# Four gates of the third branch computed among the mixer's last products, and a scan paced by 15, 13 and 9 dense products

## The chip, the core and the metric

The kernel runs on one core of a Trainium2 chip. The metric is the device time of one execution in microseconds. Every duration below comes from one execution taken by the hardware profiler, in which each engine's instructions have a start and a length. TensorE is PE in the profile, VectorE DVE, ScalarE ACT, GpSimd POOL, and SyncE, which only issues transfers here, SP.

## The reference, cut to what matters

The program is a trunk of two layers over 512 positions of width 1024. Each layer is a half-step feed-forward block, a mixer, and a second half-step feed-forward block. The change lies in the mixer:

```python
h = _rmsnorm(x, mix_norm[l])
proj = h @ w_in[l]
y_a = _deltanet_branch(...) @ w_proj_a[l]
y_b = _pooling_branch(...) @ w_proj_b[l]
y_c = _dilated_branch(...) @ w_proj_c[l]
gates = jax.nn.sigmoid(h @ w_gate[l] + b_gate[l]).reshape(B_, S, N_BRANCHES, D)
merged = gates[:, :, 0] * y_a + gates[:, :, 1] * y_b + gates[:, :, 2] * y_c
x = x + merged @ w_out[l]
```

The three gates depend on h alone, so they can be computed at any time of the mixer. Branch A is a gated delta rule in 8 chunks of 64 positions, in both directions: a scan, in which each chunk reads a state, solves a small triangular system, and writes the state.

## The kernel before, in words

Activations are kept transposed: 8 blocks of 128 features by 512 positions. Every large product is done in three passes, since each operand is split into a high part (fp32r) and the remainder: `gemm` (L222 to L239) issues for each inner block of 128 a product of high by high, high by low and low by high, L232, L234 and L236, and so an output block with 8 inner blocks takes 24 products of 128x128 by 512 columns. These are the dense products. The weights come by DMA from SP's queue (L199) and are split by `split` (L182 on ACT, L183 on DVE). The results land in three accumulators in turn, each free again when DVE has read it.

In the mixer the order of work is that of the code, as a scheduler places it on each engine:

- first the projections and preparations of the deltanet, then the 8 gates of branch A, which stay in the tiles `mg`, then 16 gates of branches B and C, each written to the DRAM tensor `gd` (L1053), then four products for z;
- then, by the string `ORDER`, the attention's projections `p0`, `p1`, `p2` with rotary additions on POOL (`rope`, L794 to L803), the attention groups `a0` to `a2`, the pooling `P`, the product `y` of branch A, and the attention's merge `m`;
- then the blocks: 8 for branch B (weights wpb, 12 products each) and 8 for branch C (wpc, 6 products each). Each reads its gate back from `gd` (L1086), multiplies on DVE (L1088) and adds to `mg` on POOL (L1089);
- then `mg` is split into the tiles MR (L182, L183), and the 8 wo products of 24 products follow (L1100), which need all eight MR.

The scan's small products don't stand by themselves. They are a list of steps, X.steps, and `step`, called after every dense product, takes the next one from the list when enough dense products have gone by: `DPACE`, 14, for each. The steps start in the middle of the gates (`MG`): five of preparation, then for each of the 8 chunks read (products L672, results used by L679 on DVE and L688 on ACT), solve (L699; L706 on ACT, L708 on DVE) and write (L716; L726 on DVE). Behind them come `out_block` (L735, L737, L740), `out_norm` (L747 to L753, with a square root and so a load of ACT's function table, L261) and `out_head` (transposes L759, then L762 and a split). In `a0` the scores (L869) go through L881, L884, L886 and the exponentials L889 before they are transposed (L899).

## Time and profile before

| what | value |
|---|---|
| median of 3 runs | 2594.52 us (2593.94 to 2596.76) |
| the profiled execution | 2593.36 us |
| its span, first to last instruction | 2591.6 us |
| granted TensorE clock, mean | 0.998 |
| PE busy | 2565.7 us, 99% |
| DVE busy | 1469.1 us, 57% |
| ACT busy | 1008.9 us, 39% |
| POOL busy | 162.3 us, 6% |

Busy time of PE is the union of durations that overlap: a dense product lasts 0.39 us, and the next may start before it ends. So the starts of the products tell more than their lengths. In a row of the timeline the bracket tells how long the engine sat idle before the instruction, and what ended that.

### The profile page before, as it was taken

To read this page: it belongs to the slowest core of one execution; us is meant where nothing else is said; L and a number is where in the kernel's file an instruction comes from. 1 tells how busy PE (TensorE), PEld (TensorE's weight loads), DVE (VectorE), ACT (ScalarE), POOL (GpSimd) and SP (SyncE) were. 2 spreads that over 40 slices of the span, in tenths; PEclk is the share of its full clock that TensorE was granted. 3 is DMA by queue.
4 is the path that set the end of the run, shared out by engine and by line. 5 is a ranking of instruction groups with operands and counts; after the bars stand their busy time and mean duration, and the time that the engine had idled before them with its cause. 6 is when DMAs were issued, how large, how long until landed. Compare 5 with 4: busy or idle time off the path is not lost.

```text
span 2591.6 us, 34050 instructions
## 1 busy us (share of the span) xinstructions
PE 2565.7 (99%) x13064; PEld 2102.1 (81%) x13064; DVE 1469.1 (57%) x2698; ACT 1008.9 (39%) x1948; POOL 162.3 (6%) x117
## 2 busy tenths in 40 slices
PE   9999999999999999999999999999999999999998
PEld 7888887888887788888888888878888877888887
DVE  6444349956757754444444443599466487544433
ACT  5333234564434333333233332355644343333322
POOL 1000000000230300000000000000012203000010
PEclk9999999999999999999999999999999999999999
DMA  4223333332432522233322333323334325322232
GB/s 154 97 98 96 112 111 98 99 118 87 122 103 74 171 91 96 97 98 96 100 96 94 97 101 114 112 89 106 107 98 121 92 74 175 98 96 94 94 98 82
DMA packets 96979, 269.36 MB, mean 104 GB/s; under 512 B 15664, under 2 KB 20144, under 8 KB 96816
## 3 DMA queue, kind: packets, MB, share of 16 engines
q1 hardware_dynamic: 75280, 229.39, 28.2%
q10 hardware_dynamic: 21536, 37.80, 4.5%
q8 instruction: 102, 1.67, 0.3%
q14 instruction: 61, 0.50, 0.1%
HBM read 243.99 MB, written 16.86 MB: 101 GB/s over the span
## 4 chain that ended last, share of the span: by engine, by line
PE 95%; DVE 2%; ACT 1%; issue 1%; DMA 1%; POOL 0%; SPq 0%; DVEq 0%; ACTq 0%
PE acc L236 29%; PE acc L232 29%; PE acc L234 29%; PE m L914 1%; PE m L672 1%; PE m L699 1%; PE m L716 1%; PE m L735 1%; PE m L899 1%; PE m L869 0%; DMA raw<-in_wo_dram 0%; DVE wl L183 0%; PE m L647 0%; PE m L1023 0%; PE m L608 0%
## 5 line engine op out<-in xcount | busy, mean ns | idle before, releaser
L182 ACT ACTIVATE wh<-raw 128x512 fp32r<-128x512 f32 (+1 forms) x870 | 539.1, 620 | 1193.0 <-PE acc L234 1068.7
L234 PE MATMUL acc<-xl,wh 128*128 128x512 f32 x2400 | 941.9, 393 | 1.4 <-DVE xl L1126 1.2
L236 PE MATMUL acc<-xh,wl 128*128 128x512 f32 x2400 | 941.7, 392 | 1.4 <-DVE wl L183 1.4
L232 PE MATMUL acc<-xh,wh 128*128 128x512 f32 x2400 | 941.1, 392 | 1.3 <-ACT wh L182 1.1
L183 DVE TENSOR_TENSOR wl<-raw,wh 128x512 fp32r<-128x512 f32 (+1 forms) x870 | 606.0, 697 | 578.1 <-ACT wh L182 572.1
L232 PEld LDWEIGHTS acc<-xh,wh 128*128 128x128 f32 x2400 | 450.9, 188 | 99.1 <-issue 3.0
L234 PEld LDWEIGHTS acc<-xl,wh 128*128 128x128 f32 x2400 | 450.9, 188 | 96.9 <-DVE xl L1126 3.9
L236 PEld LDWEIGHTS acc<-xh,wl 128*128 128x128 f32 x2400 | 451.0, 188 | 96.7 <-DVE wl L183 2.3
L232 PE MATMUL acc<-r,wh 128*128 128x512 f32 x970 | 379.8, 392 | 5.8 <-DVE f L1088 4.5
L234 PE MATMUL acc<-r,wh 128*128 128x512 f32 x970 | 378.5, 391 | 3.5 <-DVE r L183 3.5
L236 PE MATMUL acc<-r,wl 128*128 128x512 f32 x970 | 377.7, 390 | 0.0
L232 PEld LDWEIGHTS acc<-r,wh 128*128 128x128 f32 x970 | 182.1, 188 | 46.5 <-ACT r L182 4.4
L234 PEld LDWEIGHTS acc<-r,wh 128*128 128x128 f32 x970 | 182.2, 188 | 42.5 <-DVE r L183 5.8
L236 PEld LDWEIGHTS acc<-r,wl 128*128 128x128 f32 x970 | 182.1, 188 | 37.5
L298 DVE TENSOR_TENSOR t<-acc,R 128x512 f32<-128x512 f32 x88 | 60.9, 692 | 132.2 <-PE acc L236 132.2
L294 DVE TENSOR_TENSOR f<-acc,R 128x512 f32<-128x512 f32 x88 | 60.9, 692 | 128.1 <-PE acc L236 128.0
L182 ACT ACTIVATE r<-t 128x512 fp32r<-128x512 f32 x96 | 60.6, 632 | 132.6 <-DVE t L299 127.4
L183 DVE TENSOR_TENSOR r<-t,r 128x512 fp32r<-128x512 f32 x96 | 66.2, 692 | 60.8 <-ACT r L182 60.8
L579 POOL MEMSET r<- 128x1024 f32 x2 | 1.9, 953 | 1107.7 <-PE acc L236 1107.7
L365 DVE SCALAR_TENSOR_TENSOR f<-t,cw,f 128x512 f32<-128x512 f32 x96 | 69.2, 741 | 0.0
L295 ACT ACTIVATE f<-f 128x512 f32<-128x512 f32 x88 | 55.6, 632 | 23.0 <-DVE f L294 22.9
L299 DVE TENSOR_TENSOR t<-t,f 128x512 f32<-128x512 f32 x88 | 60.4, 686 | 1.3 <-ACT f L295 1.3
(282 smaller groups left out, 1744.6 us busy)
## 6 DMA issues: line engine op xcount, KB each, us to landing
raw<-in_win_dram SPq DMA_DIRECT2D x76, 512.0 KB, 3.7
raw<-in_wgt_dram SPq DMA_DIRECT2D x48, 512.0 KB, 3.3
raw<-in_f2g_dram SPq DMA_DIRECT2D x44, 512.0 KB, 3.2
raw<-in_f2u_dram SPq DMA_DIRECT2D x44, 512.0 KB, 3.3
raw<-in_f1g_dram SPq DMA_DIRECT2D x43, 512.0 KB, 3.3
raw<-in_f1u_dram SPq DMA_DIRECT2D x43, 512.0 KB, 3.3
raw<-in_f1d_dram SPq DMA_DIRECT2D x32, 512.0 KB, 3.5
raw<-in_f2d_dram SPq DMA_DIRECT2D x32, 512.0 KB, 3.4
```

The costliest lines, as they stand in the source:

```text
L182: S.activation(h, raw, AF.Copy)
L183: V.tensor_tensor(out=l, in0=raw, in1=f32(h), op=ALU.subtract)
L232: PE.matmul(acc, a, h, start=(k == 0), stop=False)
L234: PE.matmul(acc, a, l, start=False, stop=False)
L236: last = PE.matmul(acc, b, h, start=False, stop=(k == nk - 1))
L294: V.tensor_tensor(out=g1, in0=g, in1=R, op=ALU.mult)
L295: S.activation(g1, g1, AF.Silu)
L298: V.tensor_tensor(out=u1, in0=u, in1=R, op=ALU.mult)
L299: V.tensor_tensor(out=u1, in0=u1, in1=g1, op=ALU.mult)
L365: V.scalar_tensor_tensor(out=a, in0=cp[:, j:j + T], scalar=w[:, j:j + 1], in1=a, op0=ALU.mult, op1=ALU.add)
L672: PE.matmul(p1[:, h * P:(h + 1) * P], KQ[h][:, c * P:(c + 1) * P], X.ST[:, di * T + h * P:di * T + (h + 1) * P], start=True, stop=True)
L699: PE.matmul(P3[di][r0:r0 + 64, h * P:(h + 1) * P], M[di][r0:r0 + 64, o:o + 64], U[b][r0:r0 + 64, di * T + h * P:di * T + (h + 1) * P], sta ...
```

## The change

Of the 16 gates of branches B and C the first 12 are computed and written to `gd` as before. The last four, of branch C, blocks 4 to 7, are computed in the last loop, each just in front of the wpc block that uses it, and stay in the tile `t`. The two loops over the blocks become one loop over the string `YORD`, in the same sequence. The pace of the scan is given with each step: 15 dense products ahead of a read, 13 ahead of a solve, 9 ahead of a write, and 14 for all others.

```diff
-DPACE = 14
+NG = 4
+YORD = "10 11 12 13 14 15 16 17 20 21 22 23 24 25 26 27"
+DPACE = {"read": 15, "solve": 13, "write": 9}
...
-    gd = pd.tile([2 * NB, P, T], F32, name="gd")
+    gd = pd.tile([NB + NG, P, T], F32, name="gd")
...
-                if ln[1] >= ln[2]:
+                if ln[1] >= (ln[0][0][0] or ln[2]):
                     ln[1] = 0
-                    ln[0].pop(0)()
+                    ln[0].pop(0)[1]()
...
-        def add(*fs):
-            X.steps.append(lambda: [f() for f in fs])
+        def add(*fs, n=14):
+            X.steps.append((n, lambda: [f() for f in fs]))
...
-                add(lambda s=s: read(s))
-            add(lambda s=s: solve(s))
+                add(lambda s=s: read(s), n=DPACE["read"])
+            add(lambda s=s: solve(s), n=DPACE["solve"])
...
-        for d in range(2 * NB):
+        for d in range(NB + NG):
...
-        for br, yy, wp in ((0, YB, "wpb"), (1, YC, "wpc")):
-            for d in range(NB):
-                t = tf()
-                nc.scalar.dma_start(t, gd[br * NB + d])
-                y = gemm(A[wp][l][d], yy)
-                V.scalar_tensor_tensor(out=t, in0=t, scalar=1.0, in1=y, op0=ALU.add, op1=ALU.mult)
-                G.tensor_tensor(out=mg[d], in0=mg[d], in1=t, op=ALU.add)
+        for br, d in [(int(c[0]), int(c[1])) for c in YORD.split()]:
+            yy, wp = ((YB, "wpb"), (YC, "wpc"))[br - 1]
+            t = tf()
+            if br == 2 and d >= NG:
+                gate(2, d, t)
+            else:
+                nc.scalar.dma_start(t, gd[(br - 1) * NB + d])
+            y = gemm(A[wp][l][d], yy)
+            V.scalar_tensor_tensor(out=t, in0=t, scalar=1.0, in1=y, op0=ALU.add, op1=ALU.mult)
+            G.tensor_tensor(out=mg[d], in0=mg[d], in1=t, op=ALU.add)
```

How instructions move is shown at three places of the first layer. In the new file lines up to the pace's are 2 higher and those of the last loop 5 (L183 is L185, L1088 is L1093).

The first place is DVE at the last wpc blocks. `f` is a gate's tile, `wl` a low part of weights, `r<-mg` the split of the merged tiles. Before, from the fourth block on:

```order
L1088 SCALAR_TENSOR_TENSOR f_7536<-f_7536,acc_7538 128x512
L183 TENSOR_TENSOR wl_7608<-raw_7609,wh_7607 128x256
L183 TENSOR_TENSOR r_7638<-mg_3771,r_7638 128x512
L183 TENSOR_TENSOR wl_7625<-raw_7626,wh_7624 128x256
L1088 SCALAR_TENSOR_TENSOR f_7553<-f_7553,acc_7555 128x512
L1088 SCALAR_TENSOR_TENSOR f_7570<-f_7570,acc_7572 128x512
L183 TENSOR_TENSOR r_7641<-mg_3809,r_7641 128x512
L183 TENSOR_TENSOR wl_7666<-raw_7667,wh_7665 128x512
L1088 SCALAR_TENSOR_TENSOR f_7587<-f_7587,acc_7589 128x512
L183 TENSOR_TENSOR r_7644<-mg_3847,r_7644 128x512
```

And after, where L1042 takes a gate from its accumulator:

```order
L1042 TENSOR_TENSOR f_7414<-acc_7415,R 128x512
L185 TENSOR_TENSOR wl_7507<-raw_7508,wh_7506 128x256
L1093 SCALAR_TENSOR_TENSOR f_7414<-f_7414,acc_7452 128x512
L185 TENSOR_TENSOR wl_7523<-raw_7524,wh_7522 128x512
L185 TENSOR_TENSOR r_7638<-mg_3923,r_7638 128x512
L185 TENSOR_TENSOR wl_7541<-raw_7524,wh_7540 128x512
L1042 TENSOR_TENSOR f_7467<-acc_7468,R 128x512
L185 TENSOR_TENSOR wl_7560<-raw_7561,wh_7559 128x256
L1093 SCALAR_TENSOR_TENSOR f_7467<-f_7467,acc_7505 128x512
L185 TENSOR_TENSOR wl_7576<-raw_7577,wh_7575 128x512
L185 TENSOR_TENSOR r_7641<-mg_3961,r_7641 128x512
```

Between two multiplies stand now a gate's accumulator and its two weight splits of 512 columns, and one split of mg.

The second place is ACT behind the scan, where the sums of squares of the last blocks (`ocol`) are followed by the load of the function table for the square root. Before:

```order
L740 ACTIVATE t_5681,ocol_3770<-r_4651 128x128 x4
L182 ACTIVATE wh_5826<-raw_5828 128x512
L740 ACTIVATE t_5704,ocol_3770<-r_4652 128x128 x4
L761 DMA t_5780<-zd 128x512
L261 ACT_TABLE_LOAD
L261 ACTIVATE rs_994_5731<-ov_5727 128x16
L794 ACTIVATE f_5746<-acc_5648 128x512
```

And after:

```order
L742 ACTIVATE t_5633,ocol_3770<-r_4651 128x128 x4
L184 ACTIVATE wh_5785<-raw_5769 128x512
L742 ACTIVATE t_5656,ocol_3770<-r_4652 128x128 x4
L837 ACTIVATE r_5570<-m_5667 64x128
L836 ACTIVATE t_5571<-m_5668 64x128
L839 ACTIVATE r_5570<-m_5667 128x3x128
L263 ACT_TABLE_LOAD
L263 ACTIVATE rs_991_5698<-ov_5694 128x16
L184 ACTIVATE wh_5854<-raw_5856 128x512
```

The square root stood beside the rotary step of the keys; now it stands behind the copies of the first half of the values V.

The third place is PE at the transposes of the deltanet's output (L759, after the change L761), of which the two heads' banks `m` are filled in turn. Before:

```order
L236 MATMUL acc_5756<-xh_95,wl_5798 128x512
L759 MATMUL m_5775<-ident,r_4651 128x128
L759 MATMUL m_5786<-ident,r_4651 128x128
L232 MATMUL acc_5756<-xh_96,wh_5797 128x512
L234 MATMUL acc_5756<-xl_104,wh_5797 128x512
L236 MATMUL acc_5756<-xh_96,wl_5798 128x512
L232 MATMUL acc_5756<-xh_97,wh_5797 128x512
L759 MATMUL m_5775<-ident,r_4651 128x128
```

And after:

```order
L761 MATMUL m_5729<-ident,r_4651 128x128
L761 MATMUL m_5740<-ident,r_4651 128x128
L234 MATMUL acc_5766<-xh_90,wh_5767 128x512
L761 MATMUL m_5729<-ident,r_4651 128x128
L761 MATMUL m_5740<-ident,r_4651 128x128
L236 MATMUL acc_5766<-xl_98,wh_5767 128x512
L238 MATMUL acc_5766<-xh_90,wl_5768 128x512
L832 MATMUL m_5753<-ident,f_5751 64x128
```

They now come where `p0` ends and `p1` begins, among the transposes of V (L830 to L833, now L832 to L835).

## Rows read from the trace of the kernel before

**Rows 1.** The page: the busy time of each engine, and the engines' shares of the chain that ended last.

```profile
PE 2565.7 (99%) x13064; PEld 2102.1 (81%) x13064; DVE 1469.1 (57%) x2698; ACT 1008.9 (39%) x1948; POOL 162.3 (6%) x117
...
PE 95%; DVE 2%; ACT 1%; issue 1%; DMA 1%; POOL 0%; SPq 0%; DVEq 0%; ACTq 0%
```

**Rows 2.** The waits of PE over the whole span: the waiting line and what it waited for, then us in total, how many times, and the longest. The whole list has 11 rows; the six that are left out, of 0.3 to 1.4 us in total, are those of L236 (for L183 of the weights), L286, L234 (for L1126), L280, L517 and L232 (for L1125).

```profile
PE acc L232 <- DVE f L1088: 4.5, 4, 1.3
PE acc L234 <- DVE r L183: 3.5, 4, 1.0
PE acc L232 <- ACT wh L182: 2.1, 4, 0.6
PE m L1110 <- DVE R L1107: 1.5, 1, 1.5
PE m L899 <- ACT r L889: 1.5, 2, 0.8
```

**Rows 3.** The timeline of PE in the first layer's last blocks (start in us, length in us, engine, line, operation), cut to the first wpc product, one 24 products on, the last three products that waited, the first product of wo block 2, and the first product behind the wo blocks.

```profile
873.58 0.39 PE L232 MATMUL acc<-r,wh 128*128 128x512 f32 x1
...
879.02 0.39 PE L232 MATMUL acc<-r,wh 128*128 128x512 f32 x1
...
890.72 0.47 PE L232 MATMUL acc<-r,wh 128*128 128x512 f32 x1 [0.96 <-DVE f L1088]
...
892.92 0.50 PE L234 MATMUL acc<-r,wh 128*128 128x512 f32 x1 [1.04 <-DVE r L183]
...
894.61 0.50 PE L234 MATMUL acc<-r,wh 128*128 128x512 f32 x1 [0.73 <-DVE r L183]
...
901.91 0.39 PE L232 MATMUL acc<-r,wh 128*128 128x512 f32 x1
...
934.55 0.39 PE L232 MATMUL acc<-xh,wh 128*128 128x512 f32 x1
```

**Rows 4.** The first wpc product and the first product of wo block 2 in the second layer's timeline.

```profile
2157.45 0.39 PE L232 MATMUL acc<-r,wh 128*128 128x512 f32 x1
...
2185.49 0.39 PE L232 MATMUL acc<-r,wh 128*128 128x512 f32 x1
```

**Rows 5.** From 850 to 902 us the group of L1088; from 873.5 to 902 us the group of POOL's additions, and the splits of the merged tiles on ACT and DVE (shortest/median/longest in ns).

```profile
L1088 DVE SCALAR_TENSOR_TENSOR f<-f,acc 128x512 f32<-128x512 f32 x16 | 10.9, 683 | 9.8 <-POOL mg L1089 5.1 <-PE acc L236 2.2 <-PE acc L234 1.6
...
L1089 POOL TENSOR_TENSOR mg<-mg,f 128x512 f32<-128x512 f32 x9 | 13.6, 1531 | 7.1 <-DVE f L1088 7.1
...
L182 ACT ACTIVATE r<-mg x8: 612/630/635, 877.9 to 894.0; 128x512 fp32r<-128x512 f32 x8
L183 DVE TENSOR_TENSOR r<-mg,r x8: 677/682/1778, 879.2 to 896.3; 128x512 fp32r<-128x512 f32 x8
```

**Rows 6.** The timeline of the scan: a solve followed by a write, where the room between them was least, and a read followed by a solve, where the room was least.

```profile
637.45 0.68 DVE L708 TENSOR_TENSOR r<-m,Dc 64x512 f32<-64x512 f32 x1
639.78 0.49 PE L716 MATMUL m<-r,r 64*128 64x128 f32 x4
...
620.28 0.90 DVE L679 SCALAR_TENSOR_TENSOR r<-m,nsc,r 64x128 f32<-64x128 f32 x3
621.39 0.87 PE L699 MATMUL m<-r,r 64*64 64x128 f32 x12
```

**Rows 7.** The timeline behind the scan: the last sums of products, a split beside a rotary addition of POOL, the table load, the first scaling of the output and the first transposes.

```profile
671.28 3.71 PE L735 MATMUL m<-r,r 64*64 64x128 f32 x64
676.61 1.19 DVE L183 TENSOR_TENSOR wl<-raw,wh 128x512 fp32r<-128x512 f32 x1 [0.88 <-ACT wh L182]
677.76 1.28 ACT L261 ACT_TABLE_LOAD   x1
681.30 0.69 DVE L753 TENSOR_TENSOR r<-r,rs 128x512 f32<-128x512 f32 x1
682.81 0.38 PE L759 MATMUL m<-ident,r 128*128 128x128 f32 x2
```

**Rows 8.** The timeline where `p0` ends: the dense products around a group of V transposes, the first and the last copy of V, and in `a0` the end of the first exponentials and the first transposes behind them.

```profile
698.19 0.39 PE L232 MATMUL acc<-xh,wh 128*128 128x512 f32 x1
698.53 0.30 PE L830 MATMUL m<-ident,f 128*64 128x128 f32 x1
...
699.02 0.48 PE L234 MATMUL acc<-xl,wh 128*128 128x512 f32 x1
...
699.19 0.27 ACT L835 ACTIVATE r<-m 64x128 f32<-64x128 f32 x1 [1.07 <-PE m L832]
...
699.52 0.48 ACT L837 ACTIVATE r<-m 128x384 f32<-128x384 f32 x1
...
706.30 0.19 ACT L889 ACTIVATION_READ_ACCUMULATOR r<-r,nbt 128x1 f32 x1
709.43 0.60 PE L899 MATMUL m<-ident,r 128*64 128x128 f32 x4
```

**Rows 9.** A group of DVE from 656 to 700 us, one of POOL over the whole span (count, busy us, mean ns, idle us before), and a read followed by a solve beside a rotary step.

```profile
L762 DVE SCALAR_TENSOR_TENSOR t<-m,on,t 128x512 f32<-128x512 f32 x4 | 3.0, 745 | 0.9 <-DMA t<-zd 0.9
...
L803 POOL TENSOR_TENSOR r<-r,f 128x512 f32<-128x512 f32 x24 | 38.2, 1590 | 1.9
...
662.87 2.32 DVE L679 SCALAR_TENSOR_TENSOR r<-m,nsc,r 64x128 f32<-64x128 f32 x8
666.83 1.09 PE L699 MATMUL m<-r,r 64*64 64x128 f32 x16
```

More of the change, by code (lines that the diff above doesn't have):

```diff
@@ L204, in trunk @@
     units = []
-    lanes = {"d": [[], 0, DPACE], "a": [[], 0, 0]}
+    lanes = {"d": [[], 0, 0], "a": [[], 0, 0]}
     def step():
@@ L211, in step @@
                 ln[1] += 1
-                if ln[1] >= ln[2]:
+                if ln[1] >= (ln[0][0][0] or ln[2]):
                     ln[1] = 0
-                    ln[0].pop(0)()
+                    ln[0].pop(0)[1]()
     def drain(k, left=0):
         while len(lanes[k][0]) > left:
-            lanes[k][0].pop(0)()
+            lanes[k][0].pop(0)[1]()
     def queue_behind(ins, unit):
@@ L776, in deltanet @@
             if s:
-                add(lambda s=s: read(s))
-            add(lambda s=s: solve(s))
+                add(lambda s=s: read(s), n=DPACE["read"])
+            add(lambda s=s: solve(s), n=DPACE["solve"])
             if s == 5:
-                add(lambda: write(5), lambda: out_block(1), lambda: out_block(2))
+                add(lambda: write(5), lambda: out_block(1), lambda: out_block(2), n=DPACE["write"])
             elif s < 7:
-                add(lambda s=s: write(s))
+                add(lambda s=s: write(s), n=DPACE["write"])
         X.rest = 4
@@ L1069, in mixer @@
                 drain("d", X.rest)
-                lanes["a"][0].extend(attend(int(tok[1])))
+                lanes["a"][0].extend((0, f) for f in attend(int(tok[1])))
                 lanes["a"][1:] = [0, int(tok[3:])]
```

## The prediction

> **What bounds the kernel now.** I read the page first: its line of busy times puts TensorE at 99% of the span and the chain that ended last gives PE 95% of it [rows 1], so only what TensorE waits for can move the time much. Then TensorE's own list of waits: it names no line of the scan (L672, L699, L716 are absent), and its largest entries are L1088, the merge's multiply, and L183, the split; L899, 1.5 us, is a wait of the last attention blocks, which stay where they are [rows 2]. Then, in order of time, TensorE's products where the wpc blocks end and the wo products begin. The reader is to look at starts, not at durations: a dense product lasts 0.39 us but the next starts 0.227 us later. From 873.58 to 879.02 lie 24 products, 5.44 / 24 = 0.2267 us each; this holds again from 901.91 to 934.55 (32.64 / 144). But from 873.58 (wpc block 0) to 901.91 (wo product 2) there are 48 + 48 = 96 products, worth 96 x 0.2267 = 21.76 us, and they take 28.33: 6.57 us too many [rows 3]. In the second layer it is 2185.49 - 2157.45 = 28.04, so 6.28 too many [rows 4]. Together **12.85 us**, 0.5% of the time, in two places of 28 us. The rest of the list is the opening, the norms and the values of the deltanet, which the change doesn't touch.
>
> The Trainium skill ("Trainium Kernel Development and Optimization", section Performance Expectations) says that matmul busy time is a bad measure of how near a kernel is to its limit, because matmuls overlap. The trace agrees: TensorE's idle time on L1088, on L183 of r and on L182 is 4.5 + 3.5 + 2.1 = 10.1 us at most in both stretches [rows 2], where the starts give 12.85. By idle time alone the sum below would be 2.75 smaller; I go by the starts.
>
> Why TensorE waits there: a wpc block is six products, 1.36 us. Each needs a weight split, the multiply L1088 on DVE and the addition L1089 on POOL, and POOL's additions average 1.53 us in this stretch [rows 5]: POOL cannot keep up with 1.36 us. From the sixth block on, the delay goes round: L1088 waits, so its accumulator is not free, so a product waits; then the splits of mg into MR come late (up to 1.78 us on DVE beside POOL against a median of 0.68), and the wo product's inner blocks wait for them one by one [rows 3, 5].
>
> **The change part by part.**
>
> *Gates 4 to 7 of the third branch move* from the front of the mixer to the place in front of wpc blocks 4 to 7. Their 4 x 24 = 96 dense products a layer cost 0.2267 us each in both places. What they do is to space the last four blocks 30 products, 6.80 us, apart. POOL needs 1.53 of these, and the accumulator, the f tiles and the splits of mg[0] to mg[6] all come in time: in DVE's new order each split of mg stands behind its own block's multiply and a weight split, beside the next gate's products. What is late next is the last block's chain: product 0.39, L1088 0.68, addition 1.53, ScalarE's split 0.63, DVE's split 0.68 [rows 5], 3.91 us in all, against 22 products of wo 0 that don't need it, 4.99 us. The cover is about 1 us; without it the chain costs what it exceeds. So both stretches should run at 0.2267: **-12.85**, with 0 to 0.5 a layer left (the rows of before show 0.73 to 1.05 for one late split); I take 0.15 a layer, +0.3. What the gates add beside it (each an evacuation on DVE, a tanh on ScalarE, two weight splits) fits beside their 5.44 us of products, as it does in front now, where TensorE waits for none of it [rows 2]. The tanh now follows the softmax's exp; no table load stands before it in ScalarE's order, so nothing. Four gates a layer are no longer written to gd and read back; TensorE waits for none of these transfers [rows 2], so nothing. The load of hb for the next layer moves behind the last tanh on SP; behind it wait weights of wo 4, needed 4 x 24 products, 21.8 us, after wo begins: nothing.
>
> *The scan's pace.* It was 14 between all steps and is now 15, 13 and 9, so 272 products in place of 308 (7 reads, 8 solves, 7 writes); the steps ahead of and behind the scan keep 14. Since the gates that hid it shrink from 240 products to 144, it ends about 102 products into p0 and not 42. Slack before: write waits for L706 and L708, the later of which ended at 638.13 at its tightest, 1.65 us before L716 at 639.78 [rows 6]; five products fewer take 1.13. Solve waits for L679; at its tightest that ends at 620.28 + 0.90 = 621.18, and L699 starts at 621.39, 0.21 us later [rows 6], and one product fewer takes 0.23. Read gains 0.23. TensorE now waits for none of these, so no gain is possible; at worst one more DVE operation of 0.69 falls in front of L679 in two of the seven cycles: 1.4 a layer. The nearest row is the tight one, so I take 0.4 a layer: +0.8.
>
> *The tail of the deltanet* (sums of squares, norm, transposes L759) falls into the last products of p0. Its chain took from the last L735 (671.28 + 3.71 = 674.99) to the end of the first L753 (681.99) 7.0 us, and L759 started at 682.81 [rows 7]. Now 28 products and a group of V transposes stand between, 28 x 0.2267 + 0.6 (698.19 to 699.02, less one step) = 6.95 us, and ScalarE's copies of V (from 699.19 to 700.00, 0.81 us [rows 8]) stand in front of the table load, while L801 and a split (1.36) no longer stand in DVE's part of the chain, where one split remains. So it is even to within an operation: -0 to +1.3 a layer (a table load, 1.28); I take 0.4: +0.8.
>
> *The first scores of a0* now share DVE with four L762 (0.745) and four splits (0.682), 5.7 us that were done before [rows 5, 9]. Slack before: the first block's exponentials end at 706.49 (706.30 + 0.19), its transposes start at 709.43, so 2.9 us [rows 8]. Worst 5.7 - 2.9 = 2.8 a layer, best 0 (the scores stand later too); nearest 0 since the transposes L759 add products in between. I take 0.3: +0.6.
>
> *Groups of small products* between dense ones: 207 before and 205 after, counted over the whole of TensorE's order. A group costs two late starts: 0.34 us between the starts at 698.19 and 698.53 in place of 0.23 [rows 8], and by my estimate as much on the way back; 0.2 each, -0.4.
>
> Sum: -12.85 + 0.3 + 0.8 + 0.8 + 0.6 - 0.4 = -10.75. The profiled execution took 2593.36 (span 2591.6), 1.16 below the median of the runs; it would become 2582.6, the median 2594.52 - 10.75 = **2583.8**.
>
> **Rivals.** A difference below 0.2%, 5.2 us, is what a measurement of this kernel can't tell from none.
> (1) *Half is given back* where the scan's end, the norm and the first scores crowd p0 and p1: the upper ends 1.4 + 1.3 + 2.8 and 0.5 in the last block's chain reach 6.0 a layer; half of that is 6.0 in both, so 2594.5 - 13.2 + 6.0 = 2587.3, and at all of it 2593.3, no change. For it: tight slacks of 0.2 us. Against: in before the same steps stood beside the z products and the ropes without one wait of TensorE [rows 2], and the order was made anew with later places where operands are late (the write of step 5 stands 19 products behind its solve, not 9).
> (2) *The change doesn't do what it says at the end*: the last block's chain and POOL hold wo 0 as before. The three waits from 890.72 on are 0.96 + 1.04 + 0.73 = 2.73 of idle time [rows 3]; if they stay in both layers, 2583.8 + 5.5 = 2589.3. For it: POOL is unchanged and its last addition is as late after its block. Against: seven of the eight additions are done long before.
> (3) *Slower: POOL holds DVE beside the ropes.* Now 102 products' worth of scan and then L753, L762 and the splits lie in p0 and p1, where each rope has two POOL additions (the second 1.59 on average), and a split took 1.19 beside them, not 0.68, 1.78 at worst [rows 5, 7, 9]. The eight ropes have 16 such additions and products a layer; it decides from six a layer that hold up by 1.1 us (1.78 - 0.68) an operation on the path, 6.6 us. With half of the 16, 8.8 a layer and 17.6 in both: 2594.5 - 13.2 + 17.6 = 2598.9. For it: slack of 0.21 us bears no such block. Against: the L679 that began at 662.87, beside a rope's DMAs, ended at 665.19, 1.6 us ahead of L699 at 666.83 [rows 9].
> The Trainium skill ("SBUF — State Buffer", on the shared port pair) says that the pair is an exclusive lock and that a DVE operation with two SBUF inputs waits for a whole GpSimd operation. By it L679, L726 and L762, which read PSUM and one SBUF operand, would escape, and of what is moved the four L753 and four splits would not, which is rival 3 at its eight a layer. The 1.78 us row agrees for a split; no row here shows L679 beside a rope's addition.
>
> **How the numbers follow.** Forecast 0.62 (2580 to 2588), rival 1 0.22 (half of it above 2589.3), rival 2 0.08 (half above), rival 3 0.04, and 0.04 that more than 12.85 goes (waits I can't see in the starts). Faster by over 0.2% (below 2589.3): 0.62 + 0.11 + 0.04 + 0.04 = 0.81; slower: 0.03; within: 0.16. The range reaches up to where half of rival 1 and 2 lies, 2590, and down to 12.85 + 0.4 gained with no stall and a median 2 us lower, 2579; all that lies outside is 0.2.
>
> **What would show it.** Starts from the first wpc block to wo 2: 192 products at 0.2267, 43.5 us, in both layers, no bracket on L1088 or L183 r in TensorE's waits. L1089 of blocks 4 to 7 some 6.8 us apart. In the scan, L699 starting no sooner than 0.1 us after L679. A wait of TensorE at the first L759 or L899 shows rival 1; L183 or L753 at 1.2 us or more just before it, rival 3. I am wrong if new brackets of over 3 us a layer stand in p0 and p1.

## The result, and the profile after

The changed kernel took 2581.79 us (median of four runs, 2581.52 to 2581.97) beside 2594.23 us for the kernel before on the same chip (four runs, 2593.23 to 2596.76): a ratio of 0.995, 95% interval 0.9933 to 0.9968. The forecast was 2583.8, in a range of 2579 to 2590. The profiled execution of it took 2581.97 us with a span of 2580.2, so the span fell by 2591.6 - 2580.2 = 11.4 us, where the sum had -10.75. The two medians lie 12.4 us apart, because the profiled execution of the kernel before was 0.9 us under its median and that of the changed kernel 0.2 above.

TensorE's busy time and its list of waits after the change, which answer to [rows 1, 2]. L234, L236 and L238 are now the lines of the dense products, L761 the transposes behind the deltanet's norm, L901 the transposes of the attention.

```profile
PE 2561.7 (99%) x13064; PEld 2102.5 (81%) x13064; DVE 1460.7 (57%) x2698; ACT 1008.7 (39%) x1948; POOL 163.0 (6%) x117
...
PE acc L236 <- DVE xl L1131: 2.3, 3, 0.9
PE m L901 <- ACT r L891: 1.5, 2, 0.8
...
PE m L761 <- DVE r L755: 0.3, 2, 0.2
```

The two entries that led the list, 4.5 us on the multiply and 3.5 on the splits of mg, are gone. The first line of waits is the opening of the program; L761 is new, 0.3 us.

TensorE's timeline after the change, cut to the first wpc product, the product of wo block 0 that is the first to need the last split (ScalarE's high half of it; the next product, one step later, needs DVE's low half), and the first product of wo block 2; then the first and the last of these in the second layer. They answer to [rows 3, 4].

```profile
851.88 0.39 PE L234 MATMUL acc<-r,wh 128*128 128x512 f32 x1
...
889.28 0.39 PE L234 MATMUL acc<-r,wh 128*128 128x512 f32 x1
...
895.40 0.39 PE L234 MATMUL acc<-r,wh 128*128 128x512 f32 x1
...
2129.91 0.39 PE L234 MATMUL acc<-r,wh 128*128 128x512 f32 x1
...
2173.43 0.39 PE L234 MATMUL acc<-r,wh 128*128 128x512 f32 x1
```

895.40 - 851.88 = 43.52 us for 48 + 96 + 48 = 192 products, 0.2267 each, and 43.52 again in the second layer. Where 6.57 and 6.28 us were lost, nothing is lost now.

The same stretch by engines: two windows of the kernel before, and then two of the changed one (busy us and number of instructions of each engine, the granted clock, the DMA share, GB/s).

```profile
878.00:888.00 10.00, 7.94 (x34) 5.67 (x33) 8.19 (x11) 5.71 (x11) 6.11 (x5) 1.00 0.77 284
888.00:898.00 10.00, 7.27 (x29) 4.92 (x28) 9.17 (x12) 2.85 (x5) 4.12 (x3) 1.00 0.70 232
```

```profile
878.00:888.00 10.00, 10.00 (x46) 8.29 (x45) 5.19 (x9) 4.25 (x9) 3.21 (x2) 1.00 0.59 201
888.00:898.00 10.00, 10.00 (x46) 8.28 (x45) 6.88 (x13) 3.63 (x6) 0.00 (x0) 1.00 0.32 110
```

Read the third busy time, DVE's, in the kernel before: 8.2 and 9.2 of 10 us, more than POOL's (6.1 and 4.1). The prediction named POOL's rate as the cause, and DVE only as what comes late behind it.

Of 12.85 us regained, 11.4 reached the span. The rest was given back between the first products of the scan's preparation and the first wpb product. These are that stretch's two ends, before and after.

```profile
536.75 0.37 PE L608 MATMUL m<-r,r 32*32 32x32 f32 x6
...
851.71 0.47 PE L232 MATMUL acc<-r,wh 128*128 128x512 f32 x1
```

```profile
536.17 0.32 PE L610 MATMUL m<-r,r 32*32 32x32 f32 x4
...
830.01 0.47 PE L234 MATMUL acc<-r,wh 128*128 128x512 f32 x1
```

314.96 us became 293.84, 21.12 less, and 96 gate products fewer are worth 21.76: 0.64 us given back in this layer, and 0.72 by the same count in the other, 1.36 together. -12.85 + 1.36 = -11.49, which is the span's loss to 0.1 us.

For the experiments I use these two measures throughout. **Tail** is the time from the first wpb product to the first of wo block 4, less 0.2267 for each dense product in it. **Front** is the time from the first L608 to the first wpb product, less 0.2267 for each dense product in it; what is left are the small products and whatever TensorE lost among them. Each has a number for each layer, in us; "against before" takes the median of the kernel before that ran beside it.

| kernel | median | against before | tail | front |
|---|---|---|---|---|
| before | 2594.2 | | 6.7 / 6.4 | 100.5 / 100.6 |
| after | 2581.8 | -12.4 | 0.1 / 0.1 | 101.2 / 101.3 |
| gates only | 2584.6 | -8.9 | 0.1 / 0.1 | 102.3 / 102.3 |
| pace only | 2597.4 | +3.9 | 6.8 / 8.0 | 102.0 / 101.4 |
| pairs | 2598.0 | +4.5 | 8.8 / 9.2 | 100.6 / 100.5 |
| four additions left out | 2585.0 | -8.5 | 3.9 / 2.6 | 100.6 / 100.5 |
| splits of mg left out | 2585.1 | -8.3 | 2.5 / 2.4 | 100.6 / 100.6 |
| more f tiles | 2610.6 | +16.8 | 7.6 / 8.3 | 100.9 / 100.9 |
| one gate moved | 2594.9 | +1.4 | 7.0 / 5.4 | 102.0 / 101.4 |
| two gates moved | 2586.7 | -6.7 | 2.5 / 4.0 | 102.2 / 101.7 |
| four gates in a row | 2586.4 | -7.3 | 2.4 / 4.0 | 101.2 / 101.5 |
| four additions twice | 2591.4 | -2.0 | 4.8 / 5.2 | 101.2 / 101.2 |
| scan paced 15, 9, 5 | 2582.7 | -11.1 | 0.1 / 0.1 | 102.0 / 101.9 |
| scan begun sooner | 2585.8 | -8.0 | 0.1 / 0.1 | 102.8 / 103.3 |

Tail and front are those of the one profiled execution. With two gates and with four in a row it took 2589.0 us, 2.3 and 2.6 above the median; in both the second layer's tail is 1.5 to 1.6 longer than the first's, and there, and not in the first, the granted clock fell. With two gates:

```profile
2174.00:2179.00 5.00, 5.00 (x17) 3.92 (x16) 2.56 (x5) 1.77 (x3) 0.00 (x0) 0.66 0.46 157
```

The third number from the end is the granted clock; in the same stretch of the first layer (892 to 897 us) it is 1.00.

### The profile page after: what moved, and what is told of

Its sections match the earlier page's. It is cut to its first block, busy times and chain, and to the rows that moved or that the text cites. A ratio compares the mean times of both kernels' runs of the same rounds, so it can differ in the third digit from the quotient of the medians.

```text
span 2580.2 us, 34028 instructions
## 1 busy us (share of the span) xinstructions
PE 2561.7 (99%) x13064; PEld 2102.5 (81%) x13064; DVE 1460.7 (57%) x2698; ACT 1008.7 (39%) x1948; POOL 163.0 (6%) x117
## 5 line engine op out<-in xcount | busy, mean ns | idle before, releaser
L238 PE MATMUL acc<-xh,wl 128*128 128x512 f32 x2400 | 942.0, 393 | 1.5 <-DVE wl L185 1.5
L236 PE MATMUL acc<-xl,wh 128*128 128x512 f32 x2400 | 940.7, 392 | 2.3 <-DVE xl L1131 2.3
L234 PE MATMUL acc<-xh,wh 128*128 128x512 f32 x2400 | 940.4, 392 | 1.3 <-ACT wh L184 1.1
L185 DVE TENSOR_TENSOR wl<-raw,wh 128x512 fp32r<-128x512 f32 (+1 forms) x870 | 601.9, 692 | 562.6 <-ACT wh L184 557.9
L236 PEld LDWEIGHTS acc<-xl,wh 128*128 128x128 f32 x2400 | 450.7, 188 | 98.4 <-DVE xl L1131 3.9
L238 PEld LDWEIGHTS acc<-xh,wl 128*128 128x128 f32 x2400 | 450.7, 188 | 97.4 <-issue 2.7
L234 PEld LDWEIGHTS acc<-xh,wh 128*128 128x128 f32 x2400 | 450.7, 188 | 97.1 <-ACT wh L184 1.8
L234 PE MATMUL acc<-r,wh 128*128 128x512 f32 x970 | 379.1, 391 | 0.0
L236 PE MATMUL acc<-r,wh 128*128 128x512 f32 x970 | 378.1, 390 | 0.0
L238 PE MATMUL acc<-r,wl 128*128 128x512 f32 x970 | 377.9, 390 | 0.0
L238 PEld LDWEIGHTS acc<-r,wl 128*128 128x128 f32 x970 | 182.1, 188 | 37.8
L234 PEld LDWEIGHTS acc<-r,wh 128*128 128x128 f32 x970 | 182.1, 188 | 37.6
L236 PEld LDWEIGHTS acc<-r,wh 128*128 128x128 f32 x970 | 182.3, 188 | 37.1
L185 DVE TENSOR_TENSOR r<-t,r 128x512 fp32r<-128x512 f32 x96 | 66.4, 692 | 60.9 <-ACT r L184 60.7
L1094 POOL TENSOR_TENSOR mg<-mg,f 128x512 f32<-128x512 f32 x32 | 48.7, 1530 | 211.1 <-DVE f L1093 211.1
```

The costliest lines, as they stand in the source:

```text
L185: V.tensor_tensor(out=l, in0=raw, in1=f32(h), op=ALU.subtract)
L234: PE.matmul(acc, a, h, start=(k == 0), stop=False)
L236: PE.matmul(acc, a, l, start=False, stop=False)
L238: last = PE.matmul(acc, b, h, start=False, stop=(k == nk - 1))
L1094: G.tensor_tensor(out=mg[d], in0=mg[d], in1=t, op=ALU.add)
```

## The experiments

**The two halves of the change.** First the gates' move at the old pace:

```diff
-DPACE = {"read": 15, "solve": 13, "write": 9}
+DPACE = {"read": 14, "solve": 14, "write": 14}
```

> The change with its gates 4 to 7 in front of the last wpc blocks, but the scan's steps all 14 dense products apart again. Theory (the gates' new place alone brings the gain, and the pace only decides how crowded p0 and p1 become): the stretch from wpc block 0 to wo product 2 takes 43.5 us for 192 products in both layers, so 12.85 us less are lost there than before; the scan ends 36 products later than in the changed kernel, its last read and solve lie beside the ropes of p0, and the norm's transposes and the first scores meet, for which I add some 0.8 us a layer: 2583.4 us. Rival 1 (the pace costs as much as it saves; the 0.68 us a layer that TensorE loses around the transposes in the changed kernel come from the tighter scan): 2581.8 - 1.4 = 2580.4. Rival 2 (the new pace is what makes the move possible): several us a layer are given back beside the ropes, 2587 or more.

2584.6 us, ratio 0.9966 (0.9952 to 0.9979). The tail is clean, as the theory says, and the front costs 1.1 us a layer more than in the changed kernel. The entry of this kernel's list of TensorE's waits that names it:

```profile
PE m L761 <- DVE r L755: 2.9, 4, 0.9
```

The transposes wait 2.9 us in place of 0.3, because the scan and its norm end 36 products later and meet the first scores of `a0`. The theory held with its term too small (1.2 and 0.9 us a layer for 0.8); rival 1, that the pace costs as much as it saves, falls.

Then the pace without the move:

```diff
-NG = 4
+NG = 8
```

> The change's pace of 15, 13 and 9 alone: all 16 gates are computed in front, as before. Theory: the stretch from wpc block 0 to wo product 2 keeps its 6.57 and 6.28 us too many; the scan has slack for the tighter pace (smallest slack of a solve 0.21 us before, of a write 1.65), so nothing else changes: 2594.2 us, within 0.5. Rival 1 (the sooner end of the scan frees p0 by itself): up to 1 us a layer sooner, 2592.2. Rival 2 (the tighter scan stalls TensorE): 0.4 to 1.4 a layer, 2595.0 to 2597.0, with L699 in TensorE's list of waits.

2597.4 us, ratio 1.0015 (1.0006 to 1.0024): none of the three. The scan doesn't stall (L701 is not in the list of waits). The front gives up 1.5 and 0.8 us, 1.2 of it in idle time at L761. The tail of the second layer lost 1.6 more than before; this is its timeline in this kernel:

```profile
2178.67 0.50 PE L236 MATMUL acc<-r,wh 128*128 128x512 f32 x1 [1.03 <-DVE r L185]
...
2180.36 0.75 PE L236 MATMUL acc<-r,wh 128*128 128x512 f32 x1 [0.72 <-DVE r L185]
2180.91 0.63 PE L238 MATMUL acc<-r,wl 128*128 128x512 f32 x1
2181.33 0.63 PE L234 MATMUL acc<-r,wh 128*128 128x512 f32 x1
```

And one window of it:

```profile
2180.00:2185.00 5.00, 4.64 (x13) 3.71 (x14) 2.71 (x6) 1.17 (x3) 0.00 (x0) 0.66 0.61 192
```

Behind the second wait products start 0.42 us apart, and the granted clock is 0.66 over these 5 us: for part of them TensorE ran at 1.2 GHz and not 2.4. The kernel before has idle times of 1.04 and 0.73 at the same two places [rows 3] and a granted clock of 1.00 in its windows above, and in the second layer too. So a wait in the tail can be paid twice. In the first layer of this run the clock fell as well (0.66 from 892 to 897 us), right behind the first of the two waits; there the second wait is gone, and the tail is only 0.1 longer than before. The pace, which loses 3.9 us by itself, saves 2.8 (2584.6 - 2581.8) once the gates are moved: the two halves don't add.

**What held the tail.** The prediction's cause was POOL. Taken away for four blocks, in the kernel before:

```diff
-                G.tensor_tensor(out=mg[d], in0=mg[d], in1=t, op=ALU.add)
+                if br == 0 or d < 4:
+                    G.tensor_tensor(out=mg[d], in0=mg[d], in1=t, op=ALU.add)
```

> The kernel before, but POOL's additions of the third branch's blocks 4 to 7 are left out (those four terms are missing from the merge); everything else stands as before. Theory (POOL's additions at 1.53 us against 1.36 us of products a block are what holds the blocks and then the splits in front of wo 0): most of the 12.85 us goes, 2582 us, with no bracket on L1088 among TensorE's waits and the splits of mg near 0.68 us. Rival (the weights' splits on DVE and ScalarE, or the gates' read-back, set the blocks' pace): the brackets stay, 2590 us or more.

2585.0 us, ratio 0.9966 (0.9954 to 0.9978): between the two. 3.9 and 2.6 us of the loss remain with no addition in the last four blocks. Its waits of TensorE from 878 to 900 us:

```profile
PE acc L232 <- DVE f L1088: 1.2, 1, 1.2
PE acc L232 <- ACT wh L182: 0.7, 1, 0.7
PE acc L234 <- DVE r L183: 0.5, 1, 0.5
```

The same chain as before, only shorter: multiply, split of a weight, split of mg. POOL's last addition ends at 882.75 us, before all three. So I took the other half away, in the kernel before:

```diff
-            r = ring(F32R)
-            split(mg[d], r[:, 0:T], r[:, T:2 * T])
-            MR.append((r[:, 0:T], r[:, T:2 * T]))
+            MR.append(YB[d % 4])
```

> The kernel before, but the splits of the merged sum are left out (the wo products read the splits of the second branch's values in their place); all POOL additions stay. It is the other half of the run without four additions, which kept 2.8 to 4.1 us of the loss in each layer. Theory now (DVE is what is short in the tail: eight multiplies, eight splits of mg, ten splits of weights, and 1.1 us on top of every one that falls beside a POOL addition; the trace of before has DVE busy 21.8 of 24 us there): without the eight splits DVE has room and ScalarE no longer waits for POOL, so no loss is left: 2581.0 us. Rival (POOL's rate, 1.53 against 1.36 us a block, is what binds, as my prediction had it): the multiplies still wait for POOL to release the f tiles, some 1.4 to 2.9 us a layer stay in the wpc blocks: 2584 to 2587 us.

2585.1 us, ratio 0.9967 (0.9956 to 0.9978). The time is the rival's. There are no splits of mg to wait for, but 2.5 and 2.4 us stay, at the first products of wpc block 7 and of wo 0, where the theory had none. The multiply that frees the accumulator for the first of them had waited 2.1 us for its gate's transfer, and the one for the second stood behind a split of weights that took 1.78 us beside POOL. In the window of this kernel the DMA engines are busy all the time.

```profile
878.00:888.00 10.00, 8.11 (x35) 6.14 (x34) 7.51 (x10) 3.00 (x6) 6.13 (x6) 1.00 0.99 343
```

Part of that load is the edit's own. With no split to read mg, its tiles come free sooner, and the residual's reads with them; these are the reads issued from 876 to 890 us in the kernel before, and then in this one:

```profile
mg<-xd ACTq DMA_DIRECT2D x1, 256.0 KB, 2.7
```

```profile
mg<-xd ACTq DMA_DIRECT2D x7, 256.0 KB, 4.6
```

So neither POOL's additions nor the splits alone hold the tail. A short block gives 1.36 us, and asks more than that of two engines at once. Of POOL 1.53. Of DVE, at its undisturbed durations, a multiply 0.68, a split of mg 0.68 and a half-size split of weights 0.42, 1.78, with wo's own weights besides. It also asks a gate and weights of the DMA engines, which are busy for 0.77 and 0.70 of the two windows of the kernel before; there ScalarE's splits wait 3.7 us for weights (872 to 893 us), and in the second layer one multiply waits 1.3 us for its gate. How much of the 12.85 us is theirs isn't shown. To take one demand away shortens the chain until the next one binds.

On top of that DVE and POOL disturb each other. These are the splits on DVE in the kernel before from 878 to 897 us (count, busy us, mean ns), and its multiply over the whole span (shortest, median and longest in ns):

```profile
L183 DVE TENSOR_TENSOR r<-mg,r 128x512 fp32r<-128x512 f32 x8 | 7.9, 1015 | 0.0
L183 DVE TENSOR_TENSOR wl<-raw,wh 128x512 fp32r<-128x512 f32 x5 | 5.5, 1120 | 0.0
...
L1088 DVE SCALAR_TENSOR_TENSOR f<-f,acc x32: 672/686/691, 855.6 to 2174.7; 128x512 f32<-128x512 f32 x32
```

A split is 0.68 by itself [rows 5]; here thirteen took 13.4 us and not 8.8, so 4.5 us of DVE's 19 are time held up. The run without four additions is the control: from 882 to 897 us POOL's last addition ends within the first microsecond, and the same two kinds of split take 0.69 each.

```profile
L183 DVE TENSOR_TENSOR wl<-raw,wh 128x512 fp32r<-128x512 f32 x7 | 4.7, 686 | 0.0
L183 DVE TENSOR_TENSOR r<-mg,r 128x512 fp32r<-128x512 f32 x7 | 4.5, 686 | 0.0
```

So it is POOL's additions that hold them. The multiply, 691 ns at most in 32, is never held up. The Trainium skill ("SBUF — State Buffer", section on who interferes with whom) says that a DVE operation with two SBUF inputs and a GpSimd operation that reads SBUF exclude each other, and that one with at most one SBUF input is not concerned; the splits read two SBUF tiles and are held up by up to 1.1 us, the multiply has one operand in PSUM and escapes: the trace agrees on both.

Does any spacing do? The blocks in pairs, no gate moved:

```diff
-YORD = "10 11 12 13 14 15 16 17 20 21 22 23 24 25 26 27"
+YORD = "10 20 11 21 12 22 13 23 14 24 15 25 16 26 17 27"
```

> No gate is moved and the pace stays 14; the blocks of the merge stand in the order wpb 0, wpc 0, wpb 1, wpc 1 and so on, so that each pair has 18 products, 4.08 us, for its two POOL additions, 3.06 us by their mean of 1.53. Theory (the stall came from too little TensorE time per POOL addition in a row of six-product blocks, and any order that gives POOL its time removes it): the loss of 12.85 us goes, no gate's or scan's place is changed, so none of the 1.4 us given back around the transposes arises: 2581.4 us, with up to 1 us a layer left where the last wpc block's chain of 3.9 us meets wo 0: up to 2583.4. Rival (the gain comes from the gates themselves, their read-back through memory, or the work that lies beside their products): the stall stays, 2591 to 2594.

2598.0 us, ratio 1.0016 (1.0008 to 1.0025): slower than before, and my theory of POOL's rate falls with it. TensorE's wait in wo 0 in this kernel, and the window behind it:

```profile
895.48 0.80 PE L234 MATMUL acc<-r,wh 128*128 128x512 f32 x1 [2.71 <-ACT r L184]
...
895.00:900.00 5.00, 4.52 (x12) 3.35 (x13) 3.73 (x6) 2.21 (x4) 0.00 (x0) 0.66 0.50 156
```

Each pair has 4.08 us for 3.06 us of additions, POOL has room, and still the last split of mg is late by 2.7 us, and again the clock falls behind the wait. What DVE waits for in this kernel from 850 to 905 us points at the queues:

```profile
DVE wl L185 <- ACT wh L184: 7.9, 6, 2.0
DVE r L185 <- ACT r L184: 5.9, 3, 2.3
```

The first entry is 1.4 us in the kernel before (850 to 905 us), and the second is not in its list. The splits of mg now stand between the blocks on ScalarE too; they wait there for POOL (14.8 us in five waits), and the next weights' splits stand behind them.

Last, the way of the gates through memory. Three more f tiles let each gate be read back sooner, in the kernel before:

```diff
-    pf = ctx.enter_context(tc.tile_pool(name="pf", bufs=4))
-    pr = ctx.enter_context(tc.tile_pool(name="pr", bufs=24))
+    pf = ctx.enter_context(tc.tile_pool(name="pf", bufs=7))
+    pr = ctx.enter_context(tc.tile_pool(name="pr", bufs=22))
```

> The kernel before with seven f tiles in place of four, and two ring tiles fewer to make room; nothing is moved. A gate can then be read back three blocks sooner, before POOL releases the tile of the block four places ahead. Theory (DVE's work and the holds beside POOL are what is short; the read-back only follows): some waits of the multiplies for f go, 0.5 to 1 us a layer, the splits of mg stay late: 2592.0 us. Rival (the gates' way through memory, 0.26 MB a block behind POOL's release, sets the pace of the short blocks, and to move four gates gains because they need no read-back): most of the loss goes, 2585 us or less.

2610.6 us, ratio 1.0065 (1.0051 to 1.0078). Both missed. Most of the 17 us is lost outside the two stretches of the table, with two ring tiles fewer, and says nothing of the question. The tails are 7.6 and 8.3 against 6.7 and 6.4. In the first layer TensorE's waits for a multiply, 2.2 us before, are gone, as the theory has it, and the waits for the splits of mg grew from 1.8 to 3.2. So to read the gates back sooner takes one wait away and doesn't shorten the tail; but the splits of mg take their tiles from the ring that was cut, and the run doesn't separate the two.

**How much spacing it takes.** With two gates moved, and then with one:

```diff
-NG = 4
+NG = 6
```

> The change with gates 6 and 7 moved, at the pace 15, 13, 9. Theory: the first six wpc blocks stand in a row without a loss, as in before (its first wait came at block 6), the last two are spaced, so nothing is lost up to wo 2; the scan ends some 54 products into p0 in place of 102, and of the 0.7 us a layer that the transposes give back in the changed kernel only 0.1 to 0.3 stays: 2594.2 - 12.85 + 0.4 = 2581.8 at the least gain and 2580.8 at the best; I write 2581.0 us, 0.8 under the changed kernel. Rival (more blocks in a row make a backlog that two gaps don't clear): 0.5 to 1.5 a layer on the splits of mg, 2582.5 to 2584.5.

```diff
-NG = 4
+NG = 7
```

> The change with only gate 7 of the third branch moved, at the pace 15, 13, 9. Theory (the backlog of the short wpc blocks builds up over many blocks, and one gap of 24 products in front of the last lets DVE, ScalarE and POOL catch up): block 6 keeps its 0.3 us, the last block and wo 0 lose 0 to 0.6 a layer more, and the scan ends only about 30 products into p0, so the transposes give back 0.2 a layer in place of 0.7: 2594.2 - 12.85 + 2 x 0.6 + 0.4 = 2583.0 us. Rival (each of the last four blocks needs its own gap): half of the loss stays, 2588 us.

2586.7 us (ratio 0.9974, 0.9965 to 0.9983) and 2594.9 us (1.0007, 0.9998 to 1.0015): the theory that one or two gaps let the engines catch up fell twice, and both losses are larger than the rivals had them. The wait for the last split of mg, in wo 0, with two gates and with one:

```profile
892.01 0.49 PE L234 MATMUL acc<-r,wh 128*128 128x512 f32 x1 [1.60 <-ACT r L184]
```

```profile
893.10 0.79 PE L234 MATMUL acc<-r,wh 128*128 128x512 f32 x1 [2.38 <-ACT r L184]
```

The backlog of six or seven blocks in a row is carried over the gaps: DVE's order is fixed, the late splits stand in front of the next gate's evacuation, and so the next block's chain starts late too. With two gates, gate 7's last product ends at 884.29 us (883.90 + 0.39), and DVE takes the gate 2.8 us later, behind a split that waited:

```profile
886.45 0.69 DVE L185 TENSOR_TENSOR r<-mg,r 128x512 fp32r<-128x512 f32 x1 [1.84 <-ACT r L184]
887.06 0.68 DVE L1042 TENSOR_TENSOR f<-acc,R 128x512 f32<-128x512 f32 x1
```

Now all four gates, but in front of block 4 together:

```diff
+            if (br, d) == (2, NG):
+                for g in range(NG, NB):
+                    held[g] = tf()
+                    gate(2, g, held[g])
+            t = held[d] if br == 2 and d >= NG else tf()
...
-                gate(2, d, t)
+                pass
```

> The changed kernel with gates 4 to 7 all computed in front of wpc block 4 (96 dense products in a row), and blocks 4 to 7 then in a row, 24 products. The tail has the same products as in the change, and the same gates need no read-back. Theory (each short block needs its own gap, because multiply, addition and the two splits follow each other on DVE, POOL and ScalarE): four additions of 1.6 end 1.4 + 0.4 + 0.7 + 6.4 = 8.9 us after block 4 begins, the last splits 1.4 later, 10.3, against 5.44 + 4.99 = 10.4 that TensorE can go on; every DVE operation held beside POOL adds 1.1: 1 to 3 us a layer are lost, 2585.8 us. Rival (it is enough that the tail has 96 products more, or that four gates need no read-back): 2581.8 us.

2586.4 us, ratio 0.9975 (0.9964 to 0.9985), against 2585.8 expected. Same products, same gates without read-back, and 2.4 and 4.0 us lost in the two layers. It is the gap in front of each short block that counts.

How near is the changed kernel to the edge? The addition twice for the four blocks:

```diff
             G.tensor_tensor(out=mg[d], in0=mg[d], in1=t, op=ALU.add)
+            if br == 2 and d >= NG:
+                G.tensor_tensor(out=mg[d], in0=mg[d], in1=t, op=ALU.add)
```

> The changed kernel with POOL's addition done twice for the four blocks whose gate is moved (those four terms enter the sum twice). Theory (with 6.80 us a block POOL has room to spare, and only the last block's chain counts): three of the four doublings cost nothing; the last block's chain grows from 3.9 to 5.4 us against a cover of 5.0, so 0.5 us a layer come at wo product 22: 2582.8 us. Rival 1 (the second addition holds DVE's splits as well, 1.1 us each): up to 1.6 a layer, 2585.0. Rival 2 (POOL plays no part in it): 2581.8, as the changed kernel.

2591.4 us, ratio 0.9992 (0.9983 to 1.0001): 9.6 us lost for eight additions of 1.3, where I had expected 1.0 and at most 3.2. DVE's timeline between the multiplies of blocks 6 and 7 in this kernel:

```profile
880.38 0.69 DVE L1093 SCALAR_TENSOR_TENSOR f<-f,acc 128x512 f32<-128x512 f32 x1 [0.46 <-ACT f L1043]
...
884.88 0.69 DVE L185 TENSOR_TENSOR r<-mg,r 128x512 fp32r<-128x512 f32 x1 [3.21 <-ACT r L184]
...
886.09 0.68 DVE L1042 TENSOR_TENSOR f<-acc,R 128x512 f32<-128x512 f32 x1
...
887.57 0.69 DVE L1093 SCALAR_TENSOR_TENSOR f<-f,acc 128x512 f32<-128x512 f32 x1 [0.18 <-ACT f L1043]
```

The split of mg waits 3.21 us for the additions and ScalarE, and behind it in DVE's queue stand the evacuation of the next gate (L1042) and so that gate's tanh and multiply. That closes a loop from multiply to multiply, 7.19 us long, and the block has 6.80. The delay grows block by block, and then TensorE waits 2.7 us and goes on at the lower clock:

```profile
892.04 0.79 PE L234 MATMUL acc<-r,wh 128*128 128x512 f32 x1 [2.72 <-ACT r L184]
...
895.42 0.40 PE L236 MATMUL acc<-r,wh 128*128 128x512 f32 x1
```

Seven steps in 3.38 us, not 1.59. In the changed kernel the loop is one addition shorter. POOL's timeline there, blocks 4 to 7:

```profile
866.92 1.60 POOL L1094 TENSOR_TENSOR mg<-mg,f 128x512 f32<-128x512 f32 x1 [4.58 <-DVE f L1093]
872.74 1.61 POOL L1094 TENSOR_TENSOR mg<-mg,f 128x512 f32<-128x512 f32 x1 [4.22 <-DVE f L1093]
878.88 1.60 POOL L1094 TENSOR_TENSOR mg<-mg,f 128x512 f32<-128x512 f32 x1 [4.52 <-DVE f L1093]
885.68 1.60 POOL L1094 TENSOR_TENSOR mg<-mg,f 128x512 f32<-128x512 f32 x1 [5.20 <-DVE f L1093]
```

They start 5.8, 6.1 and 6.8 us apart (forecast: some 6.8), and POOL is idle for over 4 us ahead of each. The first distance, 872.74 - 866.92 = 5.82, is the loop's own length: 7.19 less one addition and its hand-over. Block 4's multiply still starts 1.8 us after its last product has ended (866.09 against 864.28); a loop of 5.82 in a block of 6.80 takes a microsecond off this delay each time, to 0.8 at block 5 and 0.2 at blocks 6 and 7. So the gap works by letting the delay shrink: 5.82 is below 6.80, and 7.19 is not.

**What is given back in front.** If it comes from how far the scan reaches into `p0`, a start one gate sooner should regain it:

```diff
-MG = 13
+MG = 12
```

> The changed kernel with the steps of the deltanet begun one gate, 24 products, sooner (their inputs are complete 6.6 us before the first of them in the changed kernel, and a gate is 5.4). Theory (what is given back, 0.7 us a layer at the transposes, comes from how far into the first projection the scan reaches): it ends 78 products into p0 in place of 102, and half to all of it goes: 2581.0 us. Rival (it comes from which operations happen to meet there; the runs with 54 and 30 products into p0 lost more there, 101.4 to 102.3 us of small products' time against 101.2): 2582 to 2583.5.

2585.8 us, ratio 0.9968 (0.9955 to 0.998): 4 us slower than the changed kernel, and beyond the rival's range. The tail is clean; the front costs 1.7 and 2.0 us a layer more. Its list of waits says where:

```profile
PE m L901 <- ACT r L891: 3.5, 6, 0.9
...
PE m L761 <- DVE r L755: 1.6, 2, 0.8
```

And the scan's own slack, by a tighter pace:

```diff
-DPACE = {"read": 15, "solve": 13, "write": 9}
+DPACE = {"read": 15, "solve": 9, "write": 5}
```

> The changed kernel with the scan paced 15, 9 and 5, so that its solves and writes stand 4 products, 0.91 us, sooner than in the change. It tests the term of the scan's slack: in the changed kernel TensorE's small products follow what they wait for by 0.72 to 1.43 us (solve) and 0.41 to 1.46 us (write), and nothing waits. Theory (the slack is real and is eaten one for one): the tightest solves, 0.72 to 0.83 us, and writes, 0.41 to 0.81 us, come to wait 0.1 to 0.5 us each, some 0.5 to 1.0 us a layer, and the scan ends 60 products sooner, which gives back up to 0.5 a layer at the transposes: 2582.5 us, with L701 or L718 in TensorE's list of waits. Rival 1 (the order is made anew and hides it): 2581.0 to 2581.8, no such entry. Rival 2 (a late step delays all later ones): over 3 us a layer, 2588 or more.

2582.7 us, ratio 0.9957 (0.9943 to 0.997). The time is the theory's, 2582.5, the picture is not: no line of the scan is in the list of waits. In one cycle of the layer the solve is instead cut in pieces, with dense products in between, as TensorE's timeline of this kernel shows:

```profile
618.63 1.08 PE L701 MATMUL m<-r,r 64*64 64x128 f32 x8
...
620.08 0.65 PE L701 MATMUL m<-r,r 64*64 64x128 f32 x4
620.65 0.51 PE L234 MATMUL acc<-xh,wh 128*128 128x512 f32 x1
621.09 0.65 PE L701 MATMUL m<-r,r 64*64 64x128 f32 x4
```

Three groups where there was one: by the starts of the dense products around them they cost 2.68 us beyond the dense steps, where the whole solve costs 1.11 in the changed kernel, so 1.57 more in each layer. The front grew by only 0.8 and 0.6: with the sooner end of the scan the wait at L761 is gone, and the transposes of the output and of V cost 0.4 us a layer less, as in the kernel before. What a stall would have cost is paid in changes between small and dense products; at the change's pace, 13 and 9, every solve is still one group.

## Why the prediction was right, and where it was not

The first point refers to DVE's half of the last split of mg in the changed kernel:

```profile
887.98 0.69 DVE L185 TENSOR_TENSOR r<-mg,r 128x512 fp32r<-128x512 f32 x1 [1.84 <-ACT r L184]
```

- **The tail, -12.85.** Right, by starts: -6.57 and -6.28, to the last digit that the rows show. The leftover of +0.3 was 0. The chain of the last block was mis-sized: from the start of its last product, 884.29, to the end of DVE's half of its last split, 888.67 (887.98 + 0.69), it took 4.38 us and not 3.91, since the addition takes 1.60, the multiply waits 0.2 for the gate's tanh, and the other hand-overs between engines are not free. That half is needed one product after 889.28, at 889.51, so 0.8 us were left and not 1.
- **The step "why TensorE waits there" was incomplete.** "POOL cannot keep up with 1.36 us" is true of POOL, but with four additions gone 3.9 and 2.6 us of the loss stayed, and with POOL given 4.08 us for two additions it grew. What the prediction left out is DVE's own work, 1.78 us a block, and the queues: a split that waits for POOL holds what stands behind it on DVE and ScalarE. The remedy was predicted rightly, since 24 products in front of each short block make it longer than the loop through them; had the change been pairs, or two gates, the same reasoning would have forecast a gain of 12 us, and the runs show +4.5 and -6.7.
- **The scan's pace, +0.8.** Nothing: no wait of TensorE in the scan. The slack of 0.21 us is less than one product, 0.23, and so would not have been enough; but the order was made anew, and in the changed kernel no solve starts less than 0.72 us after what it waits for. The +0.8 was a precaution, and that nothing came of it can't be read from the slack before.
- **Norm, first scores and groups, +0.8 + 0.6 - 0.4 = +1.0.** 1.36, of which 0.88 at the place named: the transposes of the deltanet's output and of V cost 0.44 us a layer more beyond the dense steps than before. TensorE is idle at L761, the new entry, for 0.3 us only. They stand in one group fewer in each layer, as counted (207 and 205), but dearer ones: in the first layer the dense products around the first two pairs start 0.72 and 0.54 us apart, and 0.37 each before. So the count of groups was right and its -0.4 wasn't. The rest, 0.2 to 0.3 a layer, is spread over other small products; the groups of the scores themselves cost the same as before, so the +0.6 for them was nothing.
- **The number.** 2583.8 against 2581.8: 0.6 of the 2.0 us lie in the sum, where +0.3 and +0.8 that didn't come stand against 0.36 too little in the front; the rest is the spread of the kernel before, whose median and profiled execution the forecast started from.
- **Rivals.** Half given back: no, 1.4 of a possible 12. The end doesn't gain: no, but with 0.8 us to spare; doubling four additions brings it back. POOL beside the ropes: no sign. The gates without the pace show how it would have begun: 2.9 us at L761 and 1.1 us a layer more in front.

## What to carry to other kernels

Where one engine seems to hold a stretch, add up what each block asks of every engine, and of the DMA engines, against the block's own time: when more than one is past the limit, taking the load off one of them moves the wait and doesn't end it; here more work of the bottleneck engine in front of each block did. In an engine with a fixed order a late operation that waits for another engine delays everything queued behind it, so a chain that crosses engines must fit into one block's time, loop included, or the delay grows from block to block (7.19 us in 6.80) instead of shrinking (5.82). Two edits that belong together are measured together and apart: here the pace alone lost 3.9 us and, with the gates moved, saved 2.8.

## What the runs showed of the hardware that was not expected

- A wait can cost more than its length. Behind idle times of 2.4 to 2.7 us in the tail (pairs, one gate, additions twice) the granted clock fell to between 0.5 and 0.7 over 5 us, and dense products started 0.43 us apart in place of 0.227. With pace only, 1.03 and 0.72 us of idle time were enough; in the kernel before, 1.04 and 0.73 at the same places were not. With two gates it fell behind 1.44 us in the second layer and not behind 1.60 in the first; with four gates in a row behind 1.99 in the second layer (0.66 from 2172 to 2177 us) and not behind 1.99 in the first. So the length of the wait doesn't decide alone; what does stays open.
- A split on DVE beside a POOL addition takes up to 1.78 us in place of 0.68 (0.69 where POOL is idle), and the multiply that reads PSUM is untouched (691 ns at most).
- More small groups cost TensorE time without any wait in its list: a solve cut in three in each layer, 1.57 us (2.68 in place of 1.11).
- The place of the scan's end matters in no simple way. Beside the changed kernel, whose scan ends some 102 products into `p0`, the runs with an end at 138 (gates only), 78 (begun sooner), 54, 30 and 6 (two gates, one gate, pace only) all cost more in front, from 0.1 to 2.0 us a layer; the kernel before, at 42 and with the old pace, cost 0.6 and 0.7 less. Which operations meet there is shown only as far as the waits on L761 and L901.
